# A four-layer transformer trunk on TensorE: 256-column products turned round in every second weight chunk, the first value weights of both column sets loaded up front, and the norm factor of the odd mixer placed between weight splits

## The chip, the cores and the metric

The kernel runs on one core of one Trainium2 chip. The metric is the device time of one execution in microseconds (us); less is better. The kernel before took 2847.97 us, the median of 3 runs.

## The reference

A residual trunk with SEQ = 256 tokens of D_MODEL = 2048 features passes through two layers. Each layer has a mixer, a cross-attention into 256 memory tokens, and a squared-ReLU MLP with 8192 hidden features; every one of them reads a root-mean-square norm of the residual and adds to it.

```python
mem_n = rms_norm(mem, mem_norm_g)
for l in range(DEPTH):                       # DEPTH = 2
    hn = rms_norm(x, mix_norm_g[l])
    if l % 2 == 0:
        x = x + even_mixer(hn, even_w_in, ...)   # value/gate, q, k, v; conv of 31 taps; differential attention; w_out
    else:
        x = x + odd_mixer(hn, odd_w_in, ...)     # y = b_gate * causal_dwconv(c_gate * u); y @ w_out
    x = x + cross_attention(rms_norm(x, xattn_norm_g[l]), mem_n, xq_w[l], xk_w[l], xv_w[l], xo_w[l])
    x = x + sq_relu_mlp(rms_norm(x, mlp_norm_g[l]), mlp_w1[l], mlp_w2[l])   # square(relu(h @ w1)) @ w2
return rms_norm(x, final_norm_g)
```

All weights and activations are float32. Nearly all the arithmetic is products of a 256 x 2048 activation with weights of 2048 rows.

## The kernel before

**Splits.** A float32 weight tile `raw` of 128 x 1024 is loaded by a DMA that SyncE issues (L188, in `weights`, or L949 in the MLP), ScalarE rounds it to the matmul's fp32r type (`whi`, a cast of about 1 us), and VectorE makes the rest `wlo = raw - whi` (about 1.2 us). Activations are held as such pairs too: `act.hi(k)` is the 256 tokens' high part of the k-th 128 features, `act.both(k)` high and low part side by side, 512 columns. One chunk of 128 output features over 2048 input features thus takes 16 products 512 columns wide, `whi` with `act.both(k)`, and 16 products 256 columns wide, `wlo` with `act.hi(k)`, all added up in one PSUM bank. The text calls them wide and narrow products. A chunk's weights come in two halves of eight products, each with its own `raw`, `whi` and `wlo`.

**Order within a chunk.** `long_run` (L219) runs wide products 0 to 14, then the 16 narrow ones, then wide product 15. `wide_piece` (L193) does the same for one half (7 or 8 wide, 8 narrow, the last wide). `long_run` is called by `proj_long` for most projections and by `Chunk.run` in the MLP and in the output projections.

**Buffers.** `wraw` holds 4 tiles `raw`, `wspl` 3 tiles `whi` and 4 tiles `wlo`; buffers are taken in turn. A cast into a `whi` tile therefore waits until the last product that reads the half three halves earlier has run. The first half of the tile is read by wide products 0 to 7, the second half by 8 to 15.

**Order on the engines.** Where `inorder` or `strict` is set, tokens fix the order of each engine's instructions to the order in which the code calls them. In the MLP (`mlp`, L1139) that holds throughout. A quarter of the 8192 hidden features is 16 chunks; iteration c of the loop at L1235 runs chunk c on TensorE and then lists the work for others: ScalarE copies half of chunk c-1 out of PSUM (`first_out`, L1163, the row `sum<-mm`), casts the two halves of chunk c+1, and squares; VectorE does the sum and the ReLU of chunk c-1 (`sum<-mm,sum`, then `sum<-sum,rb`), the two splits of chunk c+1 (`wlo<-raw,whi`), and further work that depends on c. After every four chunks it forms operands for the products that follow the 16 chunks: at c = 4, 8, 12 the pair `hid` and two additions `uu<-uu`, and at c = 5, 9, 13 two more additions (`combine`, L1183), a cast `hs<-uu` on ScalarE and a subtraction `hs<-uu,hs` on VectorE (`comb_hi`, `comb_lo`). After the 16 chunks come 8 output steps, which are not in question here. There are four quarters and two layers.

**Start.** `even_mixer` forms the values of two column sets of 512 columns with `proj_rows`: for each of 8 pieces of 256 input features, the products of the activations with `whi` and `wlo`, first all 8 pieces of set 0, then those of set 1. The input x arrives in 8 transfers, each issued ahead of one piece of set 0.

**Odd mixer.** The first four chunks of `odd_in` are run by halves with `proj_group`; the callback `mean` then computes the norm factor of x (`rrow`, a few tiny VectorE steps with a Newton iteration) in program order, and `spread` (L174) brings it to all partitions with two small products `nmb<-ident,rrow`. From there on chunks are run by `proj_long`.

Of the kernel before, what the change touches and what calls it, by code (L numbers as in the profile page):

```python
# [45 lines left out]
def trunk(ctx: ExitStack, tc: tile.TileContext, d):  # L46
    nc = tc.nc
    T, G = nc.tensor, nc.gpsimd
    inorder = [False]

    class Engine:

# [4 lines left out]
        def __getattr__(self, name):  # L57
            def call(*a, **k):
                i = getattr(self.engine, name)(*a, **k)  # L59
                if inorder[0]:  # L60
                    tc.stamp_issue_order_token(i.ins, self.token)
                return i
            return call

# [87 lines left out]
    def stage(delay, fn):  # L152
        stages.append((calls[0] + delay, fn))
# [14 lines left out]
    def mm(*a, **k):  # L168
        i = T.matmul(*a, **k)  # L169
        if strict[0]:  # L170
            ordered(i, "pe")
# [6 lines left out]
    def weights(src):  # L178
        run_later(rate[0], calls[0])
        run_stages(calls[0])  # L180
        calls[0] += 1
        raw = wraw.tile([P, 1024], F32, tag="raw", name="raw")
        hi = wspl.tile([P, 1024], F32R, tag="whi", name="whi")
        lo = wspl.tile([P, 1024], F32R, tag="wlo", name="wlo", bufs=4)
        n = 512 if calls[0] == 1 else 1024
        for i in range(0, 1024, n):
            o = slice(i, i + n)
            ordered(nc.sync.dma_start(out=raw[:, o], in_=src[:, o]), "load")  # L188
# [4 lines left out]
    def wide_piece(ps, hi, lo, act, k, first, last, between=None):  # L193


        w = [slice(j * P, (j + 1) * P) for j in range(8)]
        for j in range(7 if last else 8):
            mm(ps, hi[:, w[j]], act.both(k + j), start=first and j == 0, stop=False)
        for j in range(8):
            mm(ps[:, :S], lo[:, w[j]], act.hi(k + j), start=False, stop=False)  # L200
        if between:
            between()
        if last:
            mm(ps, hi[:, w[7]], act.both(k + 7), start=False, stop=True)

    def proj_group(srcs, act, order=(0, 1), between=None):


        pp = [ps_mm.tile([P, 512], F32, tag="mm", name="mm") for _ in srcs]
        for g in order:  # L210
            if g == order[-1] and len(srcs) > 1:
                run_stages(END)
            for src, ps in zip(srcs, pp):
                hi, lo = weights(src[:, g * 1024:(g + 1) * 1024])
                first, last = g == order[0], g == order[-1]
                wide_piece(ps, hi, lo, act, g * 8, first, last, between if last and ps is pp[-1] else None)
        return pp

    def long_run(ps, h, l, act, narrow=False):  # L219

        w = [slice(j * P, (j + 1) * P) for j in range(8)]
        if narrow:
            for k in range(16):
                for part in (act.lo, act.hi):
                    mm(ps[:, :S], h[k // 8][:, w[k % 8]], part(k), start=k == 0 and part == act.lo, stop=False)
            for k in range(16):
                mm(ps[:, :S], l[k // 8][:, w[k % 8]], act.hi(k), start=False, stop=k == 15)
            return ps
        for k in range(15):
            mm(ps, h[k // 8][:, w[k % 8]], act.both(k), start=k == 0, stop=False)  # L230
        for k in range(16):
            mm(ps[:, :S], l[k // 8][:, w[k % 8]], act.hi(k), start=False, stop=False)
        mm(ps, h[1][:, w[7]], act.both(15), start=False, stop=True)
        return ps

    def proj_long(src, act):
        ps = ps_mm.tile([P, 512], F32, tag="mm", name="mm")
        h, l = zip(*[weights(src[:, g * 1024:(g + 1) * 1024]) for g in range(2)])
        return long_run(ps, h, l, act)

    def proj(src, act):
        return proj_group([src], act)[0]
# [9 lines left out]
    def proj_rows(src, xh, xl, before=None):  # L252

        pp = [ps_mm.tile([P, 512], F32, tag="mm", name="mmr") for _ in range(2)]
        for g in range(8):
            if before:
                before(g)
            hi, lo = weights(src[:, g * 1024:(g + 1) * 1024])
            for j in range(2):
                k = g * 2 + j  # L260
                w = slice(j * 512, (j + 1) * 512)
                rows = [slice(t * P, (t + 1) * P) for t in range(2)]
                for n, (xx, ww) in enumerate(((xh, hi), (xl, hi), (xh, lo))):
                    for t in range(2):
                        mm(pp[t], xx(k)[:, rows[t]], ww[:, w], start=k == 0 and n == 0, stop=k == NC - 1 and n == 2)
        return pp

    class Act:

# [143 lines left out]
    def even_mixer():  # L413
# [7 lines left out]
        def load_x(g):  # L421
            nc.sync.dma_start(out=x[:, 2 * g:2 * g + 2], in_=d["xT"][:, 2 * g:2 * g + 2])
            for k in (2 * g, 2 * g + 1):
                xa.put_scaled(k, x[:, k], col("mix0", k))
                stage(4, lambda k=k: ss.add(x[:, k]))
            if g == 7:
                stage(6, x_rows)

        rr = {}

# [209 lines left out]
        cat_a, cat_o = ln["cat"], rr["co"]  # L640
        nxt, nss = Act(NC, "xn"), SumSq()
        cat = joined(cat_a, cat_o)
        for c, ps in enumerate(proj_group([d["even_out"][c] for c in range(3)], cat, (1, 0))):
            residual(c, ps, nxt, nss, "xat0")
        for c in range(3, NC):
# [4 lines left out]
    def odd_mixer(xa, ss):  # L650
        w = d["odd_in"]
        y, m = Act(NC, "y"), Act(NC, "mem")
        begun = [NC, 2 * NC, 0, NC + 1]
        rows = []

        def mean():
            strict[0] = True
            rows.append(rstd_rows(ss.acc, D, rows=ss.rows))

        made = dict(zip(begun, proj_group([w[c] for c in begun], xa, (1, 0), mean)))  # L660
        ready = {c: summed(made.pop(c)) for c in begun[:3]}
        made[2 * NC + 1] = proj_long(w[2 * NC + 1], xa)
        r = to_sbuf(spread(rows[0]))
        strict[0] = False

# [43 lines left out]
            V.tensor_tensor(t[:, :, 1], q, f(t[:, :, 0]), op=ALU.subtract)  # L709

        LAST = 4
        for c in range(NC - LAST):
# [143 lines left out]
    def cross(l, xa, ss, kmem):  # L856
# [47 lines left out]
        for h in range(XH):  # L904
            q = half.tile([P, 2, 4, S], F32R, tag="half", name="xq")
            for i in range(4):
                if i == 3:
                    k = split(keys[h // 2][:, h % 2], [4, S])
                s = summed(proj(d[f"xq{l}"][4 * h + i], xa))
                if r is None:  # L910
                    r = rstd(ss.acc, D)
                    strict[0] = True
                V.tensor_tensor(s, s, r, op=ALU.mult)
                A.copy(q[:, 0, i], s)
                V.tensor_tensor(q[:, 1, i], s, f(q[:, 0, i]), op=ALU.subtract)
            stage(X0, lambda h=h, q=q, k=k: scores(h, q, k))
        nxt, nss = Act(NC, "xn"), SumSq()

        for c, ps in enumerate(proj_group([d[f"xo{l}"][c] for c in range(4)], oa)):
            residual(c, ps, nxt, nss, f"mlp{l}")  # L920
        strict[0] = False
# [18 lines left out]
    class Chunk:  # L940
# [27 lines left out]
        def run(self, act, pool, tag, narrow=False):  # L968
            self.ps = long_run(pool.tile([P, 512], F32, tag=tag, name="mm"), self.h, self.l, act, narrow)

    class Step:

# [166 lines left out]
    def mlp(l, xa, ss, gname):  # L1139
# [83 lines left out]
        for qd in range(4):  # L1223
# [270 lines left out]
```

## Time and profile before

| | |
|---|---|
| median of 3 runs (lowest to highest) | 2847.97 us (2847.95 to 2849.41) |
| the profiled execution: device time, span | 2848.45 us, 2846.1 us |
| granted TensorE clock, mean | 0.999 |
| TensorE busy | 2834.7 us, 15843 products |
| VectorE busy | 2318.1 us (81%) |
| ScalarE busy | 1689.5 us (59%) |
| GpSimd busy | 78.6 us (3%) |
| DMA | 588.23 MB, 207 GB/s |

The span runs from the first to the last instruction, and 2.3 us lie around it. Busy time on TensorE counts overlapping products as one stretch, and a product's row begins where the profiler sees its operands enter; since products are pipelined, the distance from one start to the next says what a product costs, not the length of its row. A row of the timeline groups like instructions that follow each other: start, length, engine, line, operation, output <- inputs, shape, count. PE is TensorE, PEld its weight loads, DVE VectorE, ACT ScalarE, POOL GpSimd, SP SyncE; L59 is the line of the helper through which all VectorE and ScalarE instructions go, so that these are told apart by their tiles.

### The profile page before, as it was taken

Reading aid. Unit: us, or ns where it says so; the run is one execution under the profiler, and the core shown is the slowest. Engines: PE = TensorE matmul, PEld = TensorE weight load, DVE = VectorE, ACT = ScalarE, POOL = GpSimd, SP = SyncE. Lnnn points to the kernel's source line nnn. Section 1 sums busy time; section 2 is a strip of 40 time slices with the busy share of each in tenths; the row PEclk is TensorE's granted clock in tenths of the full one; section 3 lists DMA queues with packets and bytes.
Section 4 is the critical chain, followed back from the end, with each engine's and each line's share of the span. In section 5 each row is a group of like instructions: output and inputs, shape, how many; then the busy total and the mean of one; then the engine's idle time right before and its main releaser. Section 6 shows DMA issues by size and latency. Waiting matters only on the chain.

```text
span 2846.1 us, 42267 instructions
## 1 busy us (share of the span) xinstructions
PE 2834.7 (100%) x15843; PEld 2478.3 (87%) x15843; DVE 2318.1 (81%) x3602; ACT 1689.5 (59%) x2368; POOL 78.6 (3%) x107
## 2 busy tenths in 40 slices
PE   9999999999999999999999999999999999999998
PEld 8888888898888888888888888888988888888887
DVE  7899987777788888888987787888777888888888
ACT  6665445555565665656654455676556656656566
POOL 0000000000000000000000000000000000000000
PEclk9999999999999999999999999999999999999999
DMA  7455665545686786967765566994456867769676
GB/s 249 160 189 172 192 194 189 171 149 178 195 256 195 223 241 200 266 193 234 214 203 199 196 209 224 253 255 155 150 178 194 253 209 218 234 200 262 199 236 179
DMA packets 213516, 588.23 MB, mean 207 GB/s; under 512 B 18240, under 2 KB 84160, under 8 KB 213312
## 3 DMA queue, kind: packets, MB, share of 16 engines
q1 hardware_dynamic: 200064, 538.54, 58.1%
q0 software_dynamic: 12672, 46.14, 8.2%
q8 instruction: 124, 2.03, 0.3%
q10 hardware_dynamic: 576, 0.85, 0.1%
q14 instruction: 80, 0.66, 0.1%
HBM read 537.23 MB, written 2.10 MB: 189 GB/s over the span
## 4 chain that ended last, share of the span: by engine, by line
PE 97%; DMA 1%; DVE 1%; ACT 1%; issue 0%; SPq 0%; DVEq 0%; POOLq 0%; POOL 0%; ACTq 0%
PE mm L169 77%; PE p L169 13%; PE mmr L169 4%; PE pox L169 1%; PE sx L169 1%; DMA wlo<-raw 0%; PE sc L169 0%; DVE x L59 0%; DMA raw<-w 0%; ACT whi L59 0%; PE nmr L169 0%; PE po L169 0%; DVE wlo L59 0%; DMA raw<-odd_in 0%; DMA x<-xT 0%
## 5 line engine op out<-in xcount | busy, mean ns | idle before, releaser
L59 ACT CAST whi<-raw 128x1024 fp32r<-128x1024 f32 (+1 forms) x849 | 890.6, 1050 | 394.2 <-PE mm L169 297.2
L59 DVE TENSOR_TENSOR wlo<-raw,whi 128x1024 fp32r<-128x1024 f32 (+1 forms) x761 | 924.0, 1220 | 93.2 <-ACT whi L59 82.6
L169 PE MATMUL mm<-xn,whi 128*128 128x512 f32 x3840 | 938.7, 392 | 0.0
L169 PEld LDWEIGHTS mm<-xn,whi 128*128 128x128 f32 x3840 | 702.0, 188 | 133.3 <-DVE xn L59 0.6
L169 PEld LDWEIGHTS mm<-xn,wlo 128*128 128x128 f32 x3840 | 501.1, 191 | 24.0
L169 PE MATMUL mm<-xn,wlo 128*128 128x256 f32 x3840 | 509.1, 283 | 0.0
L59 ACT COPY sum<-mm 128x256 f32<-128x256 f32 x272 | 100.6, 371 | 394.5 <-PE mm L169 394.0
L169 PE MATMUL mm<-hid,whi 128*128 128x512 f32 (+1 forms) x1040 | 253.4, 386 | 0.0
L59 ACT CAST tw<-raws 128x1024 fp32r<-128x1024 f32 x160 | 160.6, 1046 | 145.1 <-DVE raws L59 141.2
L59 DVE TENSOR_TENSOR raws<-raws 128x512 f32<-128x512 f32 x320 | 220.8, 690 | 7.6
L169 PEld LDWEIGHTS mm<-hid,whi 128*128 128x128 f32 x1040 | 193.5, 188 | 36.8
L59 DVE TENSOR_TENSOR sum<-mm,sum 128x256 f32<-128x256 f32 x240 | 100.9, 421 | 146.5 <-ACT sum L59 146.2
L59 DVE TENSOR_TENSOR tw<-raws,tw 128x1024 fp32r<-128x1024 f32 x160 | 189.6, 1222 | 26.2 <-ACT tw L59 24.6
L169 PE MATMUL p<-tw,hs 128*128 128x512 f32 x720 | 189.2, 389 | 0.0
L59 DVE TENSOR_TENSOR x<-x,mm 128x256 f32<-128x256 f32 x255 | 106.9, 420 | 81.7 <-PE mm L169 77.2
L169 PEld LDWEIGHTS p<-tw,hs 128*128 128x128 f32 x720 | 135.2, 188 | 28.0
L966 POOL DMA_DIRECT2D wlo<-raw x88 | 74.9, 855 | 2550.8 <-ACT wlo L59 1847.1
L169 PEld LDWEIGHTS mm<-hid,wlo 128*128 128x128 f32 x1024 | 131.1, 191 | 5.8 <-DMA wlo<-raw 1.1
L169 PE MATMUL mm<-hid,wlo 128*128 128x256 f32 x1024 | 133.1, 283 | 0.4 <-DMA wlo<-raw 0.4
L169 PE MATMUL mm<-mem,whi 128*128 128x512 f32 x512 | 128.5, 393 | 0.0
L169 PE MATMUL mm<-o,whi 128*128 128x512 f32 x512 | 124.7, 392 | 0.0
L59 DVE TENSOR_TENSOR slo<-raws,shi 128x1024 fp32r<-128x1024 f32 x71 | 86.9, 1224 | 38.1 <-ACT shi L59 38.1
(227 smaller groups left out, 3236.6 us busy)
## 6 DMA issues: line engine op xcount, KB each, us to landing
raw<-w SPq DMA_DIRECT2D x384, 512.0 KB, 5.0
raws<-w SPq DMA_DIRECT2D x128, 512.0 KB, 5.2
raw<-odd_in SPq DMA_DIRECT2D x96, 512.0 KB, 4.6
wlo<-raw POOLq DMA_DIRECT2D x88, 512.0 KB, 7.5
raw<-even_in SPq DMA_DIRECT2D x64, 512.0 KB, 4.4
raw<-xk SPq DMA_DIRECT2D x64, 512.0 KB, 4.6
raw<-xq SPq DMA_DIRECT2D x64, 512.0 KB, 4.2
raw<-xo SPq DMA_DIRECT2D x64, 512.0 KB, 3.8
```

The source lines that it names most:

```text
L59: i = getattr(self.engine, name)(*a, **k)
L169: i = T.matmul(*a, **k)
L966: G.dma_start(out=self.l[g], in_=self.raw[g], accum_op=ALU.add)
```

## The change

**Turned chunks.** `long_run` gets an argument `turn`. Without it the order is as before. With `turn=0` a chunk runs its 16 wide products, then its 16 narrow ones; with `turn=1` it runs wide product 0, then the 16 narrow ones, then wide products 1 to 15. `proj_long` alternates 0, 1, 0, ... with a counter that is set back at `even_out`, `odd_in`, `odd_out` and `xo`, and the MLP's 16 chunks take `turn=c % 2`. That makes 110 turned chunks: 46 in `proj_long` and 8 in each of the 8 quarters of the MLP. The halves of the cross-attention's `xq` chunks are folded: the last half runs its 8 narrow products first and its 8 wide ones last, in all 32 chunks. Counting borders at which a wide product follows at least six narrow ones, 443 before had several wide products behind them and 25 a single one; with the change they are 325 and 117.

On TensorE, at the start of an MLP quarter, the order before is as follows; `hid` products are the output steps of the quarter ahead, `xn` is the normed input.

```order
L169 MATMUL mm<-hid,whi 128x512
L169 MATMUL mm<-xn,whi 128x512 x15
L169 MATMUL mm<-xn,wlo 128x256 x16
L169 MATMUL mm<-xn,whi 128x512 x16
L169 MATMUL mm<-xn,wlo 128x256 x16
```

At the same place it is now:

```order
L171 MATMUL mm<-hid,whi 128x512
L171 MATMUL mm<-xn,whi 128x512 x16
L171 MATMUL mm<-xn,wlo 128x256 x16
L171 MATMUL mm<-xn,whi 128x512
L171 MATMUL mm<-xn,wlo 128x256 x16
L171 MATMUL mm<-xn,whi 128x512 x31
```

Wide products of a turned chunk now stand behind its narrow ones, next to the wide ones of the chunk that follows, 31 in a row; between two runs of narrow products there is a single wide one. The order on VectorE, ScalarE and GpSimd in the MLP is as before.

**Start.** `even_mixer` runs piece 0 of set 0, piece 0 of set 1, then pieces 1 to 7 of set 0 and 1 to 7 of set 1, with the PSUM banks of both sets taken up front. `x_rows`, the norm factor's first step, is put off by 5 calls instead of 6, and `load_vec` comes with piece 1 of set 1. On SyncE, at the beginning of the program, the order before is as follows; `even_v` are the value weights, `xT` the input.

```order
L422 DMA x<-xT 128x512
L188 DMA raw<-even_v 128x512 x2
L422 DMA x<-xT 128x512
L188 DMA raw<-even_v 128x1024
L422 DMA x<-xT 128x512
```

At the same place it is now:

```order
L439 DMA x<-xT 128x512
L190 DMA raw<-even_v 128x512 x2
L190 DMA raw<-even_v 128x1024
L439 DMA x<-xT 128x512
L190 DMA raw<-even_v 128x1024
L439 DMA x<-xT 128x512
```

A second load of value weights has moved ahead of the second transfer of x.

**Odd mixer.** `mean` first takes the weights of the first half of the next long chunk, and a flag `among` stamps the tiny steps of the norm factor with the token of the splits, so that they keep their place between splits. On SyncE the four `memraw` loads that belong to later work come ahead of three loads of `odd_in` weights. On VectorE, in the last Newton step of the norm factor, the order before is as follows; `rs_t` and `rrow` are that step, `mf` other work, and `sum<-sum,rb` the factor's first use.

```order
L59 SCALAR_TENSOR_TENSOR rrow<-rs_t,rrow 128x2
L59 TENSOR_TENSOR wlo<-raw,whi 128x1024
L59 TENSOR_TENSOR rs_t<-rrow 128x2
L59 TENSOR_TENSOR mf<-mf 128x128
L59 TENSOR_TENSOR rs_t<-rs_t,rs_v 128x2
L59 TENSOR_TENSOR mf<-mf 128x128
L59 SCALAR_TENSOR_TENSOR rrow<-rs_t,rrow 128x2
L59 TENSOR_TENSOR mf<-mf 128x128 x2
L59 TENSOR_TENSOR wlo<-raw,whi 128x1024
L59 TENSOR_TENSOR sum<-sum,rb 128x256 x3
```

At the same place it is now:

```order
L59 TENSOR_TENSOR rs_t<-rrow 128x2
L59 TENSOR_TENSOR rs_t<-rs_t,rs_v 128x2
L59 SCALAR_TENSOR_TENSOR rrow<-rs_t,rrow 128x2
L59 TENSOR_TENSOR wlo<-raw,whi 128x1024 x3
L59 TENSOR_TENSOR mf<-mf 128x128 x4
L59 TENSOR_TENSOR sum<-sum,rb 128x256 x3
```

The norm factor stands in one piece ahead of three splits, where splits stood among its steps; the three splits follow each other.

The diff, cut to its core:

```diff
@@ wide_piece
+        if fold and last:
+            for j in range(8):
+                mm(ps[:, :S], lo[:, w[j]], act.hi(k + j), start=False, stop=False)
+            for j in range(8):
+                mm(ps, hi[:, w[j]], act.both(k + j), start=False, stop=j == 7)
+            return
@@ long_run
-        for k in range(15):
+        split = 15 if turn is None else 1 if turn else 16
+        for k in range(split):
             mm(ps, h[k // 8][:, w[k % 8]], act.both(k), start=k == 0, stop=False)
         for k in range(16):
-            mm(ps[:, :S], l[k // 8][:, w[k % 8]], act.hi(k), start=False, stop=False)
-        mm(ps, h[1][:, w[7]], act.both(15), start=False, stop=True)
+            mm(ps[:, :S], l[k // 8][:, w[k % 8]], act.hi(k), start=False, stop=split == 16 and k == 15)
+        for k in range(split, 16):
+            mm(ps, h[k // 8][:, w[k % 8]], act.both(k), start=False, stop=k == 15)
@@ proj_long
+    def proj_long(src, act, begun=()):
         ps = ps_mm.tile([P, 512], F32, tag="mm", name="mm")
+        h, l = zip(*begun, *[piece(src, g) for g in range(len(begun), 2)])
+        longs[0] ^= 1
+        return long_run(ps, h, l, act, turn=1 - longs[0])
@@ even_mixer
-                stage(6, x_rows)
+                stage(5, x_rows)
-        pps = [proj_rows(d["even_v"][0], xa.hi, xa.lo, load_x)]
-        load_vec()
-        pps.append(proj_rows(d["even_v"][1], xa.hi, xa.lo))
+        pps = []
+        for n, g in [(0, 0), (1, 0)] + [(n, g) for n in range(2) for g in range(1, 8)]:
+            if g == 0:
+                pps.append([ps_mm.tile([P, 512], F32, tag="mm", name="mmr") for _ in range(2)])
+            if n == 0:
+                load_x(g)
+            elif g == 1:
+                load_vec()
+            rows_piece(pps[n], d["even_v"][n], xa.hi, xa.lo, g)
@@ odd_mixer
         def mean():
+            pieces.append(piece(w[2 * NC + 1], 0))
             strict[0] = True
+            among[0] = True
             rows.append(rstd_rows(ss.acc, D, rows=ss.rows))
+            among[0] = False
...
-        made[2 * NC + 1] = proj_long(w[2 * NC + 1], xa)
+        made[2 * NC + 1] = proj_long(w[2 * NC + 1], xa, pieces)
@@ cross-attention, mlp
-                s = summed(proj(d[f"xq{l}"][4 * h + i], xa))
+                s = summed(proj(d[f"xq{l}"][4 * h + i], xa, True))
...
-                chunks[c].run(xa, ps_mm, "mm")
+                chunks[c].run(xa, ps_mm, "mm", turn=c % 2)
```

More of the change, by code (lines that the diff above doesn't have):

```diff
@@ L48, in trunk @@
     T, G = nc.tensor, nc.gpsimd
-    inorder = [False]
+    inorder, among = [False], [False]
     class Engine:
@@ L61, in call @@
                     tc.stamp_issue_order_token(i.ins, self.token)
+                elif among[0]:
+                    tc.stamp_issue_order_token(i.ins, "lo")
                 return i
@@ L191, in weights, with wide_piece @@
         return hi, lo
-    def wide_piece(ps, hi, lo, act, k, first, last, between=None):
+    def wide_piece(ps, hi, lo, act, k, first, last, between=None, fold=False):
         w = [slice(j * P, (j + 1) * P) for j in range(8)]
+        if fold and last:
[4 more added lines that the diff above has]
+            return
         for j in range(7 if last else 8):
@@ L204, in wide_piece, with proj_group @@
             mm(ps, hi[:, w[7]], act.both(k + 7), start=False, stop=True)
-    def proj_group(srcs, act, order=(0, 1), between=None):
+    def proj_group(srcs, act, order=(0, 1), between=None, fold=False):
         pp = [ps_mm.tile([P, 512], F32, tag="mm", name="mm") for _ in srcs]
@@ L215, in proj_group, with long_run @@
                 first, last = g == order[0], g == order[-1]
-                wide_piece(ps, hi, lo, act, g * 8, first, last, between if last and ps is pp[-1] else None)
+                wide_piece(ps, hi, lo, act, g * 8, first, last, between if last and ps is pp[-1] else None, fold)
         return pp
-    def long_run(ps, h, l, act, narrow=False):
+    def long_run(ps, h, l, act, narrow=False, turn=None):
         w = [slice(j * P, (j + 1) * P) for j in range(8)]
@@ L228, in long_run, with piece, proj @@
             return ps
-        for k in range(15):
+        split = 15 if turn is None else 1 if turn else 16
+        for k in range(split):
             mm(ps, h[k // 8][:, w[k % 8]], act.both(k), start=k == 0, stop=False)
         for k in range(16):
-            mm(ps[:, :S], l[k // 8][:, w[k % 8]], act.hi(k), start=False, stop=False)
-        mm(ps, h[1][:, w[7]], act.both(15), start=False, stop=True)
-        return ps
-    def proj_long(src, act):
+            mm(ps[:, :S], l[k // 8][:, w[k % 8]], act.hi(k), start=False, stop=split == 16 and k == 15)
+        for k in range(split, 16):
+            mm(ps, h[k // 8][:, w[k % 8]], act.both(k), start=False, stop=k == 15)
+        return ps
+    longs = [0]
+    def piece(src, g):
+        return weights(src[:, g * 1024:(g + 1) * 1024])
+    def proj_long(src, act, begun=()):
         ps = ps_mm.tile([P, 512], F32, tag="mm", name="mm")
[L238 to L242, printed above, removed]
+        h, l = zip(*begun, *[piece(src, g) for g in range(len(begun), 2)])
+        longs[0] ^= 1
+        return long_run(ps, h, l, act, turn=1 - longs[0])
+    def proj(src, act, fold=False):
+        return proj_group([src], act, fold=fold)[0]
     def summed(ps, out=None):
@@ L250, in summed, with proj_rows, rows_piece @@
         return out
-    def proj_rows(src, xh, xl, before=None):
+    def proj_rows(src, xh, xl):
         pp = [ps_mm.tile([P, 512], F32, tag="mm", name="mmr") for _ in range(2)]
         for g in range(8):
[L256 to L265, printed above, removed]
-        return pp
+            rows_piece(pp, src, xh, xl, g)
+        return pp
+    def rows_piece(pp, src, xh, xl, g):
+        hi, lo = weights(src[:, g * 1024:(g + 1) * 1024])
+        for j in range(2):
+            k = g * 2 + j
+            w = slice(j * 512, (j + 1) * 512)
+            rows = [slice(t * P, (t + 1) * P) for t in range(2)]
+            for n, (xx, ww) in enumerate(((xh, hi), (xl, hi), (xh, lo))):
+                for t in range(2):
+                    mm(pp[t], xx(k)[:, rows[t]], ww[:, w], start=k == 0 and n == 0, stop=k == NC - 1 and n == 2)
     class Act:
@@ L642, in even_mixer @@
         cat = joined(cat_a, cat_o)
+        longs[0] = 0
         for c, ps in enumerate(proj_group([d["even_out"][c] for c in range(3)], cat, (1, 0))):
@@ L653, in odd_mixer @@
         begun = [NC, 2 * NC, 0, NC + 1]
-        rows = []
+        longs[0] = 0
+        rows, pieces = [], []
         def mean():
+            pieces.append(piece(w[2 * NC + 1], 0))
             strict[0] = True
+            among[0] = True
             rows.append(rstd_rows(ss.acc, D, rows=ss.rows))
+            among[0] = False
         made = dict(zip(begun, proj_group([w[c] for c in begun], xa, (1, 0), mean)))
         ready = {c: summed(made.pop(c)) for c in begun[:3]}
-        made[2 * NC + 1] = proj_long(w[2 * NC + 1], xa)
+        made[2 * NC + 1] = proj_long(w[2 * NC + 1], xa, pieces)
         r = to_sbuf(spread(rows[0]))
@@ L711, in odd_mixer @@
         LAST = 4
+        longs[0] = 0
         for c in range(NC - LAST):
@@ L917, in cross @@
         nxt, nss = Act(NC, "xn"), SumSq()
+        longs[0] = 0
         for c, ps in enumerate(proj_group([d[f"xo{l}"][c] for c in range(4)], oa)):
@@ L966, in lo_added, with run @@
             G.dma_start(out=self.l[g], in_=self.raw[g], accum_op=ALU.add)
-        def run(self, act, pool, tag, narrow=False):
-            self.ps = long_run(pool.tile([P, 512], F32, tag=tag, name="mm"), self.h, self.l, act, narrow)
+        def run(self, act, pool, tag, narrow=False, turn=None):
+            self.ps = long_run(pool.tile([P, 512], F32, tag=tag, name="mm"), self.h, self.l, act, narrow, turn)
     class Step:
```

## The prediction

> **What bounds the kernel now.** I read the page's busy times first, then the chain of waits, then the waits of TensorE.
>
> ```profile
> PE 2834.7 (100%) x15843; PEld 2478.3 (87%) x15843; DVE 2318.1 (81%) x3602; ACT 1689.5 (59%) x2368; POOL 78.6 (3%) x107
> PE 97%; DMA 1%; DVE 1%; ACT 1%; issue 0%; SPq 0%; DVEq 0%; POOLq 0%; POOL 0%; ACTq 0%
> PE rest L108 <- DVE zero L59: 1.5, 1, 1.5
> PE mm L169 <- DMA wlo<-raw: 0.4, 1, 0.4
> PE nmb L174 <- DVE rrow L59: 0.3, 1, 0.3
> ```
>
> TensorE is busy for the whole span, and its three listed waits add up to 2.2 us. No product goes away with the change. So it can gain in two ways only: a smaller distance between one product's start and the next, or less waiting at the few places where TensorE waits. It can lose wherever a turned chunk wants its weights sooner than they come. Below, each distance is the difference of two start times in the timeline, divided by the count of products between them.
>
> The rows for these distances are TensorE's in the first MLP, in its output steps, and at a place in the cross-attention where a single wide product stands between narrow ones.
>
> ```profile
> 919.72 2.08 PE L169 MATMUL mm<-xn,wlo 128*128 128x256 f32 x16
> ...
> 947.55 2.08 PE L169 MATMUL mm<-xn,wlo 128*128 128x256 f32 x16
> ...
> 1000.37 0.84 PE L169 MATMUL p<-tw,hs 128*128 128x512 f32 x3
> ...
> 1007.17 2.08 PE L169 MATMUL mm<-hid,wlo 128*128 128x256 f32 x16
> 1009.08 0.40 PE L169 MATMUL mm<-hid,whi 128*128 128x512 f32 x1
> ...
> 558.30 0.40 PE L169 MATMUL mm<-xn,whi 128*128 128x512 f32 x1
> 558.54 3.05 PE L169 MATMUL pox<-pb,hl 128*128 128x256 f32 x24
> ...
> 561.42 1.99 PE L169 MATMUL mm<-xn,whi 128*128 128x512 f32 x8
> ```
>
> From 1000.37 to 1007.17 stand 30 wide products without a narrow one: 6.80/30 = 0.2267 us each. The narrow run at 1007.17 takes 1.91 us, 0.12 each. Five chunks lie between 919.72 and 947.55: 27.83/5 = 5.566 us per chunk, where 16 x 0.2267 + 16 x 0.12 = 5.547. So a border with several wide products behind it costs about 0.019 us. With a single wide product in between, 558.30 to 561.42 is 3.12 us against 0.2267 + 24 x 0.12 = 3.107: at most 0.013.
>
> **The order within chunks.** 118 full borders go (443 - 325) and 92 single ones come (117 - 25). The gain is 118 x 0.019 = 2.24 us, less 92 times something between 0 and 0.013; with the middle, 0.007, that is 0.64, so **-1.6 us**, and -1.0 to -2.3 at the ends. The Trainium skill ("TensorE: Matmul & The Clock Gate", sections "LDWEIGHTS (loading the stationary operand)" and "Back-to-back issue gap") speaks against this term: a 128-column load takes P/1.2, 107 ns, and an isolated 256-column product N/2.4 + 2.5, 109 ns, so a narrow product would cover the load behind it and a border would cost nothing; by that estimate the term is 0 instead of -1.6. The trace does not agree: a narrow product takes 120 ns, and a chunk 19 ns more than its products.
>
> **The start.** The rows are those of the second value piece; `mmr` are value products, PEld their weight loads.
>
> ```profile
> 7.38 0.33 SPq L188 DMA_DIRECT2D raw<-even_v  x1
> ...
> 9.12 0.61 PE L169 MATMUL mmr<-wlo,xn 128*128 128x512 f32 x2
> ...
> 9.64 1.23 DVE L59 TENSOR_TENSOR wlo<-raw,whi 128x1024 fp32r<-128x1024 f32 x1 [0.21 <-ACT whi L59]
> 9.66 0.76 PEld L169 LDWEIGHTS mmr<-whi,xn 128*128 128x128 f32 x4 [0.35 <-ACT whi L59]
> 9.66 1.20 PE L169 MATMUL mmr<-whi,xn 128*128 128x512 f32 x4
> ...
> 10.92 0.30 PEld L169 LDWEIGHTS mmr<-wlo,xn 128*128 128x128 f32 x2 [0.50 <-DVE wlo L59]
> 10.92 0.73 PE L169 MATMUL mmr<-wlo,xn 128*128 128x512 f32 x2
> ...
> 11.49 1.09 PE L169 MATMUL mmr<-whi,xn 128*128 128x512 f32 x4
> ```
>
> Eight products begin between 9.12 and 11.49, 2.37 us for 8 x 0.2267 = 1.81: TensorE loses 0.55 us to a cast and a split that are late. With piece 0 of the other column set here, 12 more products (2.7 us) use activations already made, and the splits catch up. I take the whole **-0.55**, and -0.3 at the other end, if the load of the added piece comes late. On SyncE one load of weights now passes ahead of x's second transfer, an issue of 0.33 us; the products that need that transfer come 2.7 us later, so it is hidden. If that cover were gone, it would cost the 0.33.
>
> **The odd mixer.** First the wait for the norm factor, then the third chunk run by `proj_long` after it.
>
> ```profile
> 1444.88 0.39 PE L169 MATMUL mm<-xn,whi 128*128 128x512 f32 x1
> ...
> 1445.61 0.41 PE L174 MATMUL nmb<-ident,rrow 128*128 128x128 f32 x2 [0.34 <-DVE rrow L59]
> ...
> 1447.64 6.67 SPq L188 DMA_DIRECT2D raw<-odd_in  x3
> ...
> 1456.77 3.82 PE L169 MATMUL mm<-xn,whi 128*128 128x512 f32 x16
> 1457.20 1.06 ACT L59 CAST whi<-raw 128x1024 fp32r<-128x1024 f32 x1 [1.66 <-PE mm L169]
> ...
> 1457.60 1.21 DVE L59 TENSOR_TENSOR wlo<-raw,whi 128x1024 fp32r<-128x1024 f32 x1
> ```
>
> From the wide product at 1444.88 to `nmb` 0.73 us pass, where 0.23 would do. With the factor in one piece ahead of the splits the wait goes: **-0.50** (-0.3 at the least, the wait that the trace names).
>
> Against it stands a new wait. The three splits now follow the factor, and the first uses of it follow them; `proj_long` turns every second chunk. The chunk whose first wide product starts at 1456.77 + 0.23 = 1457.00 is turned, and wants its first narrow half one product later, at 1457.23. The split for it ends at 1457.60 + 1.21 = 1458.81. That is 1.6 us late by before's times, at a place where VectorE is behind with the factor's uses. The new order lets some of those splits go earlier. I take **+0.9**, between 0 and 1.7. The four `memraw` issues that pass ahead of three loads of `odd_in` are inside this range: SyncE stands 6.67 us over three issues there, waiting for free tiles, more than four issues of 0.33.
>
> **Folds and other long chunks.** In a folded piece the narrow products come 7 products (1.6 us) sooner; the split must be done by the piece's start.
>
> ```profile
> 565.03 1.22 DVE L59 TENSOR_TENSOR wlo<-raw,whi 128x1024 fp32r<-128x1024 f32 x1
> ...
> 569.79 1.78 PE L169 MATMUL mm<-xn,whi 128*128 128x512 f32 x7
> ```
>
> The split for the piece at 569.79 ends at 566.25, 3.5 us ahead: no cost. Without that cover each of 32 folds could cost up to 1.2, one split. The turned chunks of `even_out`, `xo` and `odd_out` are alike, and cost nothing.
>
> **The MLP, the main term.** The rows run from chunk 5 of a quarter to chunk 7: the rows of TensorE whose first product ends one chunk and whose other 15 begin the next; the splits for chunk 6 and 7; and the work between them on VectorE.
>
> ```profile
> 927.20 3.82 PE L169 MATMUL mm<-xn,whi 128*128 128x512 f32 x16
> ...
> 929.24 2.54 DVE L59 TENSOR_TENSOR wlo<-raw,whi 128x1024 fp32r<-128x1024 f32 x2
> 929.47 1.06 ACT L59 CAST whi<-raw 128x1024 fp32r<-128x1024 f32 x1 [0.52 <-PE mm L169]
> ...
> 931.70 0.88 DVE L59 TENSOR_TENSOR uu<-uu 128x256 f32<-128x256 f32 x2
> 932.61 1.05 ACT L59 CAST hs<-uu 128x1024 fp32r<-128x1024 f32 x1 [1.77 <-DVE uu L59]
> ...
> 933.69 1.22 DVE L59 TENSOR_TENSOR hs<-uu,hs 128x1024 fp32r<-128x1024 f32 x1 [1.12 <-ACT hs L59]
> ...
> 934.84 0.42 DVE L59 TENSOR_TENSOR sum<-mm,sum 128x256 f32<-128x256 f32 x1
> ...
> 935.29 0.43 DVE L59 SCALAR_TENSOR_TENSOR sum<-sum,rb 128x256 f32<-128x256 f32 x1
> 935.63 2.35 DVE L59 TENSOR_TENSOR wlo<-raw,whi 128x1024 fp32r<-128x1024 f32 x2
> ...
> 938.33 3.82 PE L169 MATMUL mm<-xn,whi 128*128 128x512 f32 x16
> ```
>
> Chunk 5 starts at 927.20 + 0.23 = 927.43, chunk 7 at 938.33 + 0.23 = 938.56. The cast at 929.47 is the second half of chunk 6. It waits for TensorE, because with three `whi` tiles it takes the tile of chunk 5's first half, whose last reader is wide product 7, 1.59 us into the chunk (7 x 0.2267); the cast follows 0.45 us later. Turned, chunk 5 reads that product after 1 + 6 wide and 16 narrow ones, 0.227 + 1.91 + 6 x 0.2267 = 3.50 us in. So the cast is 1.9 us later.
>
> What stands behind that cast on VectorE? Its split (929.24 + 2.54 = 931.78), two additions (to 932.58), the cast `hs` on ScalarE (to 933.66), its subtraction (to 934.91), sum and ReLU (to 935.72), and then the two splits for chunk 7, which end at 936.85 and 937.98. Each begins within 0.1 us of the end of the one ahead. There is no slack to take up the 1.9 us, so the splits come at about 938.77 and 939.90.
>
> In the old order chunk 7 needs them after 15 wide products, at 938.56 + 3.40 = 941.96. Turned, it needs the first after one, at 938.79, and the second eight narrow products later, at 939.75. Both are thus on the edge: the first even, the second 0.15 us late. A late split costs more than the bare difference, since the weight load has to go ahead of its product: at the start above, the split ended at 9.64 + 1.23 = 10.87, its load began at 10.92, and its two products took 0.11 us longer than the two at 9.12. Each of the two is thus late by its difference plus 0.16: the first 0.14 to 0.18, the second about 0.18. I take 0.36 per place, between 0.18 (the second alone) and 0.41 (the cast 0.05 later still).
>
> ```profile
> L59 ACT CAST hs<-uu x32: 1041/1052/1054, 761.3 to 2800.6; 128x1024 fp32r<-128x1024 f32 x32
> ```
>
> The 32 casts `hs` are four per quarter, three of them inside the chunk loop, at c = 5, 9 and 13: 24 places, each with a turned chunk behind. 24 x 0.36 = **+8.6 us**, between 4.3 and 9.8. Queued behind the late cast on ScalarE is all that follows there too, but TensorE waits only for the splits.
>
> **The sum.** -1.6 - 0.55 - 0.50 + 0.9 + 8.6 = +6.85 us. The profiled execution took 2848.45, 0.48 above the median of the runs, so it goes to 2855.3, and the median to 2847.97 + 6.85 = **2854.8**. By the ends the case runs from 4.3 - 2.3 - 1.05 = +0.95 to 9.8 + 1.7 - 1.0 - 0.6 = +9.9, 2848.9 to 2857.9. About 0.2%, 5.7 us, is what a measurement of this kernel tells from no change; this forecast is just above that.
>
> **Rivals.**
>
> *The splits come in time.* It decides within 0.2 us: if the chain of VectorE closes up its little gaps, or the freed tile is seen sooner, both splits arrive before their products, and nothing stands against the gains: -1.6 - 0.55 - 0.50 = -2.65, and 2845.3 us. For it: the first split is even by my own count. Against it: 24 like places, and a chain without slack. Chance 0.25. That is not slower.
>
> *Lateness spreads.* If the chunks after 8 and 12 (9 and 13) are late as well, 16 more places at 0.36 add 5.8: 2860.6 us. Against it: there no `hs` stands between the splits, so VectorE should catch up the 1.9 us. Chance 0.10.
>
> *Turning saves nothing.* If a single wide product costs as much as a full border, the order brings 118 x 0.019 - 92 x 0.019 = 0.5 instead of 1.6: 2855.9 us. Against it speaks the 0.013 above. Chance 0.05.
>
> **How the numbers follow.** My forecast has 0.60. The range takes in it and the first rival, 2845.0 to 2858.5, and leaves out the second. Slower by over 0.2% (above 2853.7) is some 0.6 of the forecast's 0.60 = 0.36, plus both last rivals, 0.51 together. Within 0.2% are the rest of the forecast and most of the first rival: 0.46. Faster by over 0.2% needs more than twice the gains that I found: 0.03.
>
> **What would show it.** In the profile after, TensorE's waits list `mm <- DVE wlo` some 24 to 48 times, at chunks 7, 11 and 15 of each quarter, for 8 us; the cast of the second half at even chunks begins 1.9 us later; wide products stand in rows of 31, 0.2267 us apart; the waits at the value piece and at `nmb` are gone. It would be wrong if TensorE shows no wait in the MLP, or waits at other chunks.

## The result, and the profile after

The changed kernel took 2868.57 us (median of 6 runs, 2865.82 to 2869.77) against 2848.4 us (6 runs, 2847.95 to 2851.3): ratio 1.007, 95% interval [1.006, 1.0081]. It is slower by 20.2 us, where +6.85 was forecast and 2858.5 was the end of the range. The direction was right, the size was not. The profiled execution's span went from 2846.1 to 2866.8 us, +20.7.

The waits of TensorE in the changed kernel: engine, tile and what it waited for, then us in total, how often, the longest.

```profile
PE mm L171 <- DMA wlo<-raw: 10.2, 8, 1.5
PE rest L110 <- DVE zero L59: 1.5, 1, 1.5
PE mm L171 <- DVE wlo L59: 1.4, 1, 1.4
PE ptd L176 <- DVE pexp L59: 0.4, 1, 0.4
```

Half of the loss stands in the first line, and the forecast has no term for it. These are waits on a transfer, eight times, once per MLP quarter. Before, the same line read 0.4 us, once. The wait on the norm factor (`nmb <- DVE rrow`) is gone as forecast. The 24 stalls that were the forecast's main term don't appear here, since each is short; they are found in the timeline, at the place that the prediction showed, chunk 5 to chunk 7 of a quarter.

```profile
929.39 0.40 PE L171 MATMUL mm<-xn,whi 128*128 128x512 f32 x1
...
929.62 2.08 PE L171 MATMUL mm<-xn,wlo 128*128 128x256 f32 x16
...
931.54 7.25 PE L171 MATMUL mm<-xn,whi 128*128 128x512 f32 x31
933.38 1.05 ACT L59 CAST whi<-raw 128x1024 fp32r<-128x1024 f32 x1 [2.47 <-PE mm L171]
...
934.46 1.23 DVE L59 TENSOR_TENSOR wlo<-raw,whi 128x1024 fp32r<-128x1024 f32 x1 [2.04 <-ACT whi L59]
...
937.60 1.23 DVE L59 TENSOR_TENSOR hs<-uu,hs 128x1024 fp32r<-128x1024 f32 x1 [1.12 <-ACT hs L59]
...
939.54 2.36 DVE L59 TENSOR_TENSOR wlo<-raw,whi 128x1024 fp32r<-128x1024 f32 x2
...
940.54 0.39 PE L171 MATMUL mm<-xn,whi 128*128 128x512 f32 x1
940.81 2.15 PEld L171 LDWEIGHTS mm<-xn,wlo 128*128 128x128 f32 x16 [0.20 <-DVE wlo L59]
940.81 2.36 PE L171 MATMUL mm<-xn,wlo 128*128 128x256 f32 x16
...
943.01 3.36 PE L171 MATMUL mm<-xn,whi 128*128 128x512 f32 x14
```

Chunk 5 begins at 929.39. The cast of chunk 6's second half (933.38) waited 2.47 us for TensorE and comes 3.99 us into chunk 5; before it came at 929.47 - 927.43 = 2.04. That is the 1.9 us forecast. The chain behind it on VectorE is unbroken, and the splits for chunk 7 (939.54) end at 941.90, while the narrow run begins at 940.81. From its single wide product to the next wide one chunk 7 takes 943.01 - 940.54 = 2.47 us, chunk 5 takes 931.54 - 929.39 = 2.15: 0.32 us, of which 0.04 comes back in the wide run behind it. So 24 x 0.28 = 6.7 us.

Now the eight waits. They stand at the end of each quarter, in the narrow run of the first output chunk. Its `wlo` isn't made on VectorE: `lo_added` lets ScalarE write -raw, rounded to fp32r, with two scaled copies, and GpSimd then issues two transfers that add `raw` onto them, which leaves the rest. First the old kernel, the end of the first quarter: the splits for chunk 15, the two adding transfers (POOL), and the output chunk's narrow run.

```profile
808.35 2.35 DVE L59 TENSOR_TENSOR wlo<-raw,whi 128x1024 fp32r<-128x1024 f32 x2
...
814.14 1.89 POOL L966 DMA_DIRECT2D wlo<-raw  x2 [615.48 <-ACT wlo L59]
...
816.86 1.54 PE L169 MATMUL p<-sw,hid 128*128 128x512 f32 x6
...
825.06 2.18 PE L169 MATMUL mm<-hid,wlo 128*128 128x256 f32 x16
```

SyncE's queue at that time:

```profile
803.22 7.84 SPq L949 DMA_DIRECT2D raw<-w  x4
811.11 0.98 SPq L981 DMA_DIRECT2D raws<-w  x2
```

The same in the changed kernel, engines and then SyncE's queue:

```profile
810.54 2.35 DVE L59 TENSOR_TENSOR wlo<-raw,whi 128x1024 fp32r<-128x1024 f32 x2
...
814.40 1.89 POOL L996 DMA_DIRECT2D wlo<-raw  x2 [616.01 <-PE mm L171]
...
817.42 1.52 PE L171 MATMUL p<-sw,hid 128*128 128x512 f32 x6
...
826.99 2.17 PE L171 MATMUL mm<-hid,wlo 128*128 128x256 f32 x16 [1.25 <-DMA wlo<-raw]
```

```profile
803.88 9.36 SPq L979 DMA_DIRECT2D raw<-w  x4
813.30 0.98 SPq L1011 DMA_DIRECT2D raws<-w  x2
```

The four loads `raw<-w` are for the first and second output chunk; the last two of them need the tiles that chunk 15's splits set free. These splits end at 810.70 before and at 812.89 now, since chunk 15 is one of the late ones. SyncE takes its loads in turn, so the `raws` loads of a later step, which by then wait for nothing themselves, go from 811.11 to 813.30. The adding transfers start within 0.3 us of their old time (814.14 and 814.40). The loads led them by 3.03 us before and lead by 1.10 now; this lead is what the experiments below turn on. In the chain that ended last, the second adding transfer runs 11.6 us and releases the narrow run.

```profile
815.34 11.61 DMA wlo<-raw
```

### The profile page after: what moved, and what is told of

The parts are those of the page before. It is cut to its first block, busy times and chain, and to the rows that moved or that the text cites. A ratio compares the mean times of both kernels' runs of the same rounds, so it can differ in the third digit from the quotient of the medians.

```text
span 2866.8 us, 42249 instructions
## 1 busy us (share of the span) xinstructions
PE 2844.3 (99%) x15843; PEld 2477.9 (86%) x15843; DVE 2311.8 (81%) x3602; ACT 1693.1 (59%) x2368; POOL 78.6 (3%) x107
## 4 chain that ended last, share of the span: by engine, by line
PE 91%; DMA 5%; DVE 2%; issue 1%; ACT 1%; POOLq 0%; POOL 0%; DVEq 0%; ACTq 0%; SPq 0%
PE mm L171 71%; PE p L171 12%; PE mmr L171 5%; DMA wlo<-raw 3%; DMA raw<-w 1%; DVE wlo L59 1%; PE sx L171 1%; PE pox L171 1%; ACT whi L59 1%; DVE cv L59 0%; DVE sum L59 0%; DMA raw<-even_in 0%; PE nmr L171 0%; DMA raw<-odd_in 0%; PE rest L110 0%
## 5 line engine op out<-in xcount | busy, mean ns | idle before, releaser
L171 PE MATMUL mm<-hid,wlo 128*128 128x256 f32 x1024 | 133.7, 283 | 10.2 <-DMA wlo<-raw 10.2
```

## The experiments

Theory A: a turned chunk releases the `whi` tile of its first half 1.9 us later; this makes chunk 7, 11 and 15 wait for splits, and by the `raw` tiles and SyncE's queue it pushes loads into the adding transfers. Rival B: the eight waits have another cause. Rival C: it is the early wish for the splits, not the late release, that counts. The single runs are set against the medians 2848.4 and 2868.57; their first 7.5 us alone can differ by 1.5 us (see the last section). The old kernel's run beside the first four experiments took 8610.07 us, for no reason on record, and isn't used; beside the next four it took 2849.18, beside the last four 2848.56 (median of 21).

**The MLP in the old order.** One line is undone: `chunks[c].run(xa, ps_mm, "mm", turn=None)`.

> The changed kernel with the MLP's chunks in the old order; all else stays. Theory A (in a turned chunk the second half's cast for the next chunk comes 1.9 us late; this makes the splits late at three places of each quarter, 24 x 0.29 us, and by way of SyncE's queue it pushes weight loads into the accumulating transfers of the first output chunk, 8 x 1.4 us): the waits on accumulated wlo tiles and those inside narrow runs vanish, and the time is 2868.6 - 6.9 - 11.5 - 1.3 (the order itself) = about 2849. Rival B (the wait for the accumulated tiles has another cause, at the start or in the odd mixer, for example a shift against the DMA queues): about 2861.

Measured: 2850.56 us. 18.0 of the 20.2 us come from turning the MLP's chunks. Theory A's number was 1.5 us too low: three listed waits on the adding transfers are left, 1.2 us in all. The old order is near the edge here too.

**Chunk 13 not turned, and chunk 15 not turned.** The edits are `turn=c % 2 if c != 13 else 0` and the same with 15. They differ in whether chunk 15's splits come late.

> The changed kernel with chunk 13 of each quarter not turned (16 wide, 16 narrow). Theory A: the splits of chunk 15 come in time, so the loads behind them in SyncE's queue do too; all 8 long waits on accumulated wlo tiles fall to the 0.5 us or less of before, and the stalls in chunk 15 vanish, those in 7 and 11 stay: 2868.6 - 11 - 8 x 0.29 = about 2855. Rival B (the wait comes from chunk 15's own order or from something else in the output steps): the 8 waits stay near 1.4 us, and the time is about 2866.

> The changed kernel with chunk 15 of each quarter not turned; 13 stays turned. Theory A: chunk 15's stalls vanish since it wants its splits later, but the splits are as late as with the change and so are the loads behind them, so the 8 waits on accumulated wlo tiles stay or grow (TensorE arrives 0.3 us sooner): 2868.6 - 8 x 0.29 + 8 x 0.29 = between 2866 and 2869. Rival B (chunk 15's own order causes the wait): the 8 waits go, about 2855.

Measured: 2854.76 and 2873.19 us. With 13 in the old order, chunk 15 itself still turned, the waits are gone; with 15 in the old order they are worse than with the change. The rows of SyncE's step loads, the adding transfers and the output chunk's narrow run, first without 13 turned, then without 15:

```profile
811.35 0.98 SPq L1011 DMA_DIRECT2D raws<-w  x2
...
814.12 1.89 POOL L996 DMA_DIRECT2D wlo<-raw  x2 [616.04 <-ACT wlo L59]
...
825.05 2.09 PE L171 MATMUL mm<-hid,wlo 128*128 128x256 f32 x16
```

```profile
813.02 0.98 SPq L1011 DMA_DIRECT2D raws<-w  x2
...
814.11 1.89 POOL L996 DMA_DIRECT2D wlo<-raw  x2 [616.44 <-ACT wlo L59]
...
827.20 3.10 PE L171 MATMUL mm<-hid,wlo 128*128 128x256 f32 x13 [2.02 <-DMA wlo<-raw]
```

The adding transfers are issued at the same time in both. Only the lead of the step loads differs, 2.77 against 1.09 us, and with it whether TensorE waits. Rival B is out. The second run came out 4 us above the end of its range: the waits grew to 14.1 us in all, and behind two of them products ran at half speed for 3.4 us, which loses 1.7 us each time (see the last section).

**Eight wide products ahead, and five.** In the MLP's odd chunks `split` is 8, and in another kernel 5. With 8 the first half is released as in the old order; with 5 it is as late as with the change, but the splits are wanted 0.9 us later.

> The changed kernel in which the MLP's odd chunks run 8 wide, 16 narrow, 8 wide products: the first half of whi is released where it was before the change, and eight wide products stand between two narrow runs. Theory A: the cast of the next chunk's second half is in time again, all stalls in chunks 7, 11 and 15 and all 8 long waits go: about 2849, as without any turning in the MLP. Rival C (it is the closeness of narrow runs to the splits, not the release of the whi tile, that makes the splits late): splits are wanted 1.6 us later than when turned, so the stalls go, but the cast stays 1.9 us late and the 8 waits stay, about 2860.

> The changed kernel in which the MLP's odd chunks run 5 wide, 16 narrow, 11 wide products. The first half of whi is released as late as with the change (5 + 2 wide and 16 narrow products ahead), but the splits are wanted 0.9 us later. Theory A: the stalls inside narrow runs in chunks 7, 11 and 15 vanish (6.9 us), but the loads in SyncE's queue stay late, and the 8 waits on accumulated wlo tiles stay and grow by what TensorE arrives sooner: 2863 to 2869. Rival C (the waits come from the narrow run standing so near to the chunk's start): the waits shrink too, about 2852.

Measured: 2852.73 and 2867.34 us. With 8 the lead is 813.48 - 810.47 = 3.01 us, and 1.6 us of waits on adding transfers are left; stalls in narrow runs are gone. The 3.7 us above the number are these waits and some 1.5 us in the odd mixer, where products ran at half speed for a while behind the stall (see the last section). With 5 the stalls are gone too, but the lead is 1.09 us and the eight waits grow to 14.4 us. So the late release alone makes the waits, while the stalls need the early wish as well: theory A for the larger part, C for the smaller.

**The even chunks turned.** The edit is `turn=1 - c % 2`.

> The changed kernel with the even chunks of the MLP turned instead of the odd ones, so that the late casts fall on iterations without the extra work hs. Theory A: the splits have slack there, the 24 stalls vanish (6.9 us); chunk 14 is turned, its late cast makes the second split of chunk 15 and with it the loads some 1.5 us late instead of 2.2, so the 8 waits shrink but don't vanish: 2855 to 2862. Rival B (the wait belongs to a turned chunk 15): it goes wholly, 2851 or less.

Measured: 2864.89 us, above theory A's range. The 24 stalls are gone, as expected. But the lead is 815.08 - 813.75 = 1.33 us, hardly more than with the change, and the waits are 9.9 us. The cast for chunk 15 waits for turned chunk 14; the expectation took the loads to be some 1.5 us late instead of 2.2, and the lead says otherwise. Some 2.4 us more than with the change are lost in the odd mixer, where the wait is 2.1 us instead of 1.4 and 3.4 us at half speed stand behind it. Rival B falls once more, since chunk 15 isn't turned here.

**The step loads ahead of the second output chunk's loads.** Turning stays; only SyncE's order changes.

```diff
             for c in range(NC):
                 chunks[c].run(xa, ps_mm, "mm", turn=c % 2)
+                if c == 15 and seven:
+                    st[2].load()
                 fetch((Chunk, Step))
...
                     st[k].run(sevens.pp, hid, sa, k)
-                    fetch(Step)
+                    if k:
+                        fetch(Step)
```

> The changed kernel with the step loads that stand behind the second output chunk's weights in SyncE's queue issued ahead of them (first tile 5 to 7 us sooner). Theory A (these loads take DMA time from the accumulating transfers because they were pushed into them): the 8 waits shrink to 0.7 us or less, the 24 stalls stay: about 2858 to 2862. Rival D (the weight loads of the second output chunk, still late, are what collides, or the accumulating transfers are slow by themselves): the waits stay, 2867 or more.

Measured: 2858.83 us, 9.7 less than the change. All eight waits are gone, and the stalls are as they were. The waits cost more than these 9.7 us: by the distances of the starts TensorE loses 12.3 us at the eight places with the change, 0.7 before and nothing here. This kernel gives some 2.4 us of it back in the odd mixer, where the wait is 2.1 us instead of 1.4 and 3.4 us at half speed follow it.

```profile
807.60 3.13 SPq L1011 DMA_DIRECT2D raws<-w  x2
...
814.89 1.89 POOL L996 DMA_DIRECT2D wlo<-raw  x2 [616.84 <-PE mm L171]
...
826.08 2.08 PE L171 MATMUL mm<-hid,wlo 128*128 128x256 f32 x16
```

The lead is 7.3 us (of the first of the two loads, as everywhere here). The second output chunk's own loads are still late, so they alone aren't what hurts, and rival D is out. Over all fourteen kernels the lead tells the wait in this quarter: 2.8 to 3.0 us (four kernels) and 7.3 to 9.2 us (four) go with waits of 0 to 0.3 us, 1.1 to 1.3 us (six) with 1.2 to 2.4. The last link, that the two kinds of transfer share the same engines, fits what the DMA view says of this stretch: the adding transfers' median from issue to landing is 8.4 us before, 10.1 with the change, 7.5 here. In all eight quarters the second of the two adding transfers lands 8.9 to 10.5 us after its issue before, 11.0 to 11.9 with the change and 6.9 to 8.6 here. The Trainium skill ("DMA: Bandwidth & Descriptors", section "Queues, rings and completion order") says that each DMA engine goes round the queues it has work for, a packet from each; by it, loads from SyncE slow an adding transfer from GpSimd, and these times agree.

**The odd mixer in the old order.** `proj_long` gets a flag that leaves `turn` out for the chunks of `odd_in`.

> The changed kernel with the odd mixer's long chunks over odd_in in the old order (15 wide, 16 narrow, 1 wide); the norm factor stays between the splits. If the stall of 1.6 to 2.2 us in the third of them comes from the turned order, it goes and the time is 2866.3; if it comes from the new place of the norm factor and the splits behind it, it stays and the time is 2868.5.

Measured: 2866.15 us, and no wait there: the stall goes with the turned order, not with the new place of the norm factor. Its rows in the changed kernel:

```profile
1466.27 0.39 PE L171 MATMUL mm<-xn,whi 128*128 128x512 f32 x1
...
1466.81 1.22 DVE L59 TENSOR_TENSOR wlo<-raw,whi 128x1024 fp32r<-128x1024 f32 x1
...
1468.08 1.22 PE L171 MATMUL mm<-xn,wlo 128*128 128x256 f32 x8 [1.42 <-DVE wlo L59]
```

The narrow run begins 1.81 us after its wide product, where 0.23 would do: 1.6 us, behind the split that VectorE, late with the factor's uses, begins at 1466.81.

**What a border costs.** The traces so far gave a surprise. Narrow runs of pairs of chunks in the changed kernel, and in the kernel with 8 wide products ahead:

```profile
905.17 2.08 PE L171 MATMUL mm<-xn,wlo 128*128 128x256 f32 x16
907.08 0.40 PE L171 MATMUL mm<-xn,whi 128*128 128x512 f32 x1
...
927.48 2.08 PE L171 MATMUL mm<-xn,wlo 128*128 128x256 f32 x16
```

```profile
903.03 2.08 PE L171 MATMUL mm<-xn,wlo 128*128 128x256 f32 x16
...
925.30 1.96 PE L171 MATMUL mm<-xn,wlo 128*128 128x256 f32 x15
```

Two pairs take 22.31 us turned, 11.155 per pair; with 8 ahead 22.27, 11.135; in the old order a pair takes 2 x 5.566 = 11.132. Turning makes a pair 0.023 us dearer, not cheaper. In the kernel with even chunks turned, the first chunk of a quarter had by chance two wide products between narrow runs, and there it was cheaper. So two wide products were tried everywhere (`split` 2 instead of 1), by themselves, and together with the odd mixer in the old order and the step loads ahead.

> The changed kernel with two wide products instead of one ahead of the narrow run of every turned chunk (110 chunks). Theory E (the distance between two narrow runs sets the price of the border: with one wide product between them a pair of chunks took 21 ns more than in the old order, at the one place in the run with even chunks turned where two stood between, 27 ns less): the order gains 110 x 0.048 = 5.3 us against the change. The splits are wanted 0.23 us later, so the stalls fall from 0.29 us per place to 0.1 or none, another 4.5 to 6.9 us; the 8 waits on accumulated tiles grow by what TensorE arrives sooner in the quarter, up to 8 us. Together 2857 to 2864. Rival F (a border costs 27 ns however many wide products stand there, and the single one was merely unlucky): the order gives back 2.3 us at most.

> The changed kernel with two wide products ahead of the narrow run of turned chunks, the odd mixer's chunks over odd_in in the old order, and the step loads issued ahead of the second output chunk's weights. Theory A and E together: no waits on accumulated tiles, few or no stalls, no stall in the odd mixer, the order 27 ns cheaper per pair of chunks than before: 2848.4 - 0.9 (start) - 0.4 (norm factor) - 0.6 (folds) - 87 x 0.027 = 2844.1, up to 2846.5 if 0.1 us of stall is left at each of 24 places.

Measured: 2860.2 us, 8.4 less than with one; and 2846.41 us (11 runs), ratio 0.9992 [0.9983, 1.0001]. The second kernel's narrow runs:

```profile
902.16 2.08 PE L171 MATMUL mm<-xn,wlo 128*128 128x256 f32 x16
904.07 0.63 PE L171 MATMUL mm<-xn,whi 128*128 128x512 f32 x2
...
924.37 1.83 PE L171 MATMUL mm<-xn,wlo 128*128 128x256 f32 x14
```

22.21 us for two pairs, 11.105 each: 27 ns less than the old order, 50 less than with a single one. Theory E holds, F is out. Why one wide product between narrow runs is dear and two are free, no run here shows. The Trainium skill ("TensorE: Matmul & The Clock Gate", section "Back-to-back issue gap") says that the spacing is set by weight loads and products together, through a reorder window; the trace agrees in so far as the price hangs on the neighbours, 0.023 us more per pair or 0.027 less.

**Nothing turned.** All `long_run` calls in the old order, the rest of the change kept, and the step loads ahead; and the same without folds.

> All chunks in the old order (nothing turned), the start, the folds and the norm factor's place as in the change, and the step loads issued ahead of the second output chunk's weights. 2848.4 - 0.9 (start) - 0.4 (norm factor) - 0.6 (folds) - 0.6 (what before lost on accumulated tiles) = 2845.9, if the new place of the norm factor costs nothing once no chunk is turned; 2847.5 if it does.

> As the kernel with nothing turned, but without the folds in the cross-attention. A fold puts 16 narrow products together and saves one border of 27 ns in two halves; 32 folds are about 0.6 us, so the span is 0.6 us longer than that kernel's; if folds cost anything by late splits, it is shorter.

Measured: 2846.0 us (11 runs), ratio 0.999 [0.9981, 0.9999] against the old kernel's 2848.56, the one kernel of the study that is faster than before by more than its interval; and 2845.7 us in a single run, with a span of 2843.9 against 2843.2. Of these 0.7 us, 0.56 arise in the two cross-attentions: a fold saves about 0.56/32 = 0.018 us in the profile; the single time can't show that. TensorE's waits in the first of them:

```profile
PE rest L110 <- DVE zero L59: 1.5, 1, 1.5
PE mmr L171 <- ACT whi L59: 0.2, 1, 0.2
```

The new place of the norm factor costs nothing once no chunk is turned. The two-wide kernel should have been 2 to 3 us faster than this one by its order, and isn't: some 0.1 us of stall is left at each of the 24 places in the MLP (a narrow run of 1.99 us there against 1.90 elsewhere), about 2 us.

## Why the prediction was wrong

**The chain in the MLP** was right in each link: the release 1.9 us later, the unbroken chain on VectorE, the late chunks 7, 11 and 15. Its size was 24 x 0.28 = 6.7 us where +8.6 stood.

**The step that failed** is the sentence that what is queued behind the late cast matters no further, "TensorE waits only for the splits". The late splits also hold `raw` tiles; SyncE waits for these tiles, with other loads in line behind; and the delayed loads ran into the adding transfers. This cost 11.6 us (12.3 at the eight places, 0.7 before), the largest single term, where the forecast had none; the kernel with the step loads ahead, 9.7 us shorter, shows the cause. The hint was on the page: the prediction quoted `mm <- DMA wlo<-raw: 0.4` as a listed wait of the old kernel, and never asked which transfer that was. A wait of 0.4 us says that this transfer has no slack at that place; at the eight places of the old kernel the second adding transfer landed between 1.0 us ahead of its first use and 0.5 behind it. Without the eight waits the change would have cost some 9 us, 2857, inside the range, but by terms that offset each other: the order came out 3.5 us dearer than forecast and the MLP's stalls 1.9 cheaper.

**The order within chunks** had the wrong sign. The forecast took a single wide product between narrow runs as nearly free (at most 0.013 us) from one place where 24 other narrow products followed. In the turned chunks the price shows in the wide run behind: a pair costs 0.023 us more, 110 x 0.023 = +2.5 us. The folds bring -0.6. Together +1.9 instead of -1.6. The rival "turning saves nothing" was nearer, and the rule named beside the term (a border would cost nothing, so nothing could be saved) had the better result for the wrong reason, since borders do have a price: a fold removes one and saves 0.018 us, close to the 0.019 of the prediction.

**The odd mixer's new wait**, +0.9 between 0 and 1.7, was 1.6 us of stall. The kernel without it is 2.4 us shorter, but it also has some 20 turned chunks fewer (0.5 us), and its eight waits are 9.2 us instead of 10.2. The mechanism and the place were right, and the value should have been the upper end: nothing in the new order lets that split go earlier, since VectorE's work there is the same.

**The start**, -0.55, was about right. The products that began at 10.92 begin at 10.22, 0.70 sooner:

```profile
8.86 0.62 PE L171 MATMUL mmr<-wlo,xn 128*128 128x512 f32 x2
...
9.31 1.07 PE L171 MATMUL mmr<-whi,xn 128*128 128x512 f32 x4
...
10.22 0.62 PE L171 MATMUL mmr<-wlo,xn 128*128 128x512 f32 x2
```

No wait stands between these rows, and 6 products take 1.36 us. But 0.26 us of the 0.70 is there already at the first row, 8.86 against 9.12, ahead of the place in question: at the program's beginning the granted clock reads 0.50, until 7.43 us in the trace before and 6.84 in this one, and that moment differs from profile to profile whatever the kernel (see the last section). By 16 us the gain is 0.90; without the clock's share, 0.59/2 = 0.3, it is 0.6.

**The norm factor's** -0.50 is about -0.4: the changed trace's lag falls from 9.6 to 9.2 us at `nmb`.

Summed by the profiles: +1.9 (order) - 0.9 (start) - 0.4 + 1.6 + 6.7 + 11.6 = +20.5, and +20.9 with the new wait `ptd` of 0.4 us in the list, which has no explanation here; the spans differ by 20.7.

## What to carry to other kernels

When a change makes a buffer free later, follow every queue that waits for that buffer and for the ones behind it, to the end: the engine that you watch may be late by 0.3 us while a load queue passes on the whole delay to transfers that have nothing to do with it. A wait of 0.4 us on a transfer in the old profile marks a place with no slack, and belongs into the bounds of any change that moves loads. And price a new pattern of products by a place that has the whole pattern, or measure it first: one against two products between two runs changed the sign.

## What the runs showed of the hardware

The distance from one wide product to the next is 0.2267 us, and in the old kernel a run of 8, 16 or 32 narrow ones alike makes the five wide ones behind it 27 ns longer in all; with two wide ones between two narrow runs the first border's price isn't paid. And in five kernels products ran at half speed for 3.4 us, six times in all, from 0.1 to 1.5 us behind the end of a wait of 2.15 to 2.55 us (by the distance of the product starts). The granted clock reads 0.50 in these stretches and 1.00 around them; each loses 1.7 us. So it is in the kernel with five wide products ahead, from 828.55 to 831.96:

```profile
827.44 2.93 PE L171 MATMUL mm<-hid,wlo 128*128 128x256 f32 x16 [2.38 <-DMA wlo<-raw]
830.17 0.63 PE L171 MATMUL mm<-hid,whi 128*128 128x512 f32 x1
830.60 1.05 PE L171 MATMUL p<-shi,hid 128*128 128x512 f32 x2
831.45 0.63 PE L171 MATMUL p<-slo,hid 128*128 128x512 f32 x1
```

Four wide products stand 0.43 us apart there, from 830.17 to 831.88, and the narrow ones ahead of them 0.21. Waits of 2.0 us and less were not followed by that, nor were some as long or longer, 2.5 and 2.8 us in the same kernel. The clock reads 0.50 at the beginning of every profile here too, until 4.6 us in the shortest case and 7.5 in the longest: the same first products can thus take up to 1.5 us more in one profile than in another.
